# Weight tiles at eight different byte offsets in a residual block on one core

## The chip, the cores and the metric

The kernel runs on one core of one Trainium2 chip. The metric is the device time of one execution in microseconds; lower is better. TensorE (PE) multiplies, VectorE (DVE) and ScalarE (ACT) do elementwise work, GpSimd (POOL) a little of it, and SyncE (SP) issues most DMAs. PEld is TensorE's loading of the operand that stays in the array while the other streams past.

## The reference

One residual block over 256 tokens of width 1024, all in float32:

```python
h = rmsnorm(x, ffn1_pre_g)
x = x + 0.5 * rmsnorm(swiglu(h, ffn1_w_in, ffn1_w_down), ffn1_post_g)
h = rmsnorm(x, mix_pre_g)
q_a, f_a, i_a, g_a, q_b, k_b, v_b, f_b, gates = split(h @ w_in)
y_a = (rmsnorm(hgrn2_chunkwise(q_a, f_a, i_a, lb), hg_norm_g) * silu(g_a)) @ w_branch_a
y_b = fox_attention(q_b, k_b, v_b, f_b + fox_f_bias) @ w_branch_b
y = sigmoid(gate_0) * y_a + sigmoid(gate_1) * y_b
x = x + rmsnorm(y @ w_out, mix_post_g)
x = x + rmsnorm(mem_cross_attention(rmsnorm(x, mem_pre_g), rmsnorm(mem, mem_kv_g)), mem_post_g)
h = rmsnorm(x, ffn2_pre_g)
x = x + 0.5 * rmsnorm(swiglu(h, ffn2_w_in, ffn2_w_down), ffn2_post_g)
```

The two feed-forward parts have an inner width of 2816. `hgrn2_chunkwise` is a gated linear recurrence with 8 heads, `fox_attention` a causal attention with a forgetting bias and 8 heads, and the memory read has 4 heads over 256 memory rows.

## The kernel before

All weights lie in DRAM as 261 units of 128 rows by 1024 float32 words (512 KB each). `unit` (L112) brings one in: a DMA from SP's queue into a buffer `raw` (4 of these), a ScalarE copy (L121) that rounds it to the format float32r as `hi`, and a VectorE subtraction (L122) that puts the rest, raw - hi, into `lo`. There are 8 buffers each for `hi` and `lo`. These two tiles are the "two parts" of a unit. Units are numbered in the order of the table `_ORDER` (L49); most of them are asked for in fours (`chunk`, L126). The numbers run from 0 (first feed-forward block) to 260.

Activations are split in the same way and held transposed by the class `Pair` (L138): tiles `hT` and `lT` of 128 partitions with four blocks of 256 tokens. A product of activations and weights is then three matmuls per block, hi by hi, hi by lo and lo by hi, added up in PSUM. Two forms carry nearly all of them:

- weights streamed, activations loaded (`proj_tok`, L156, `act_first`, `down`, `rows_proj`): 512 columns of `hi` or `lo` stream past a loaded 128 by 128 block of `hT`, `lT` or `act`. In the rows of the profile the streamed operand stands first behind the arrow: `mm<-hi,hT ... 128x512`.
- activations streamed, weights loaded (`proj_col`, L165): 256 columns of `hT` or `lT` stream past a loaded 128 by 128 block of `hi` or `lo`: `mm<-hT,hi ... 128x256`.

Every such matmul is issued by the helper `MM` (L78 and L79), so its line is L79 whichever part of the block it belongs to. The stages run one after the other in the reference's order; small pieces of work (transposes, products of the recurrence, norms) are put at given places among the matmuls by `after` (L82), which counts issued matmuls. The gated recurrence (class `Rec`, `products` and `grow`) multiplies unrounded float32 tiles `k` and `q` in 32 by 32 pieces at the levels m = 0, 1, 2, 4, 8, 16, 32, 64 and 128; for m below 32 it takes the columns whose position has a given bit set (`odd`), so at m = 1 every second word, at m = 16 a plain run of 16 words.

The first input is X1 (L397): the tokens of x, transposed by the host and multiplied by the gain of the first norm (`gain_split`, L241), from tiles `xT` whose blocks are 257 words long because a gain stands behind each. X1 is the loaded operand in the first feed-forward block.

Data tiles of the pool `data` (tag `m4`: hT, lT, act, k, q, f and others) share 21 buffers of equal size, and a buffer has the size of the largest tile of its tag: 4096 bytes a partition. Buffers of `hi` and `lo` have 4096 bytes too. As laid out, the first `hi` buffer begins at byte 47136 of each partition, the first `lo` buffer at 79904, the first `m4` buffer at 112672, and all of these are 2080 modulo 4096.

Of the kernel before, what the change touches and what calls it, by code (L numbers as in the profile page):

```python
# [10 lines left out]
F32R = mybir.dt.float32r  # L11
# [5 lines left out]
P = 128  # L17
D = 1024
T = 256
# [24 lines left out]
WARM = 7  # L44

X_AT = 6


_ORDER = [  # L49
# [15 lines left out]
def block_kernel(ctx: ExitStack, tc: tile.TileContext, wts, x_in, xT_in, mem_in, memT_in, cols, rows, fbias, masks, out):  # L65
# [4 lines left out]
    wp = ctx.enter_context(tc.tile_pool(name="weights", bufs=4))  # L70
# [18 lines left out]
    def nm(s):  # L89
        count[0] += 1  # L90
        return f"{s}_{count[0]}"

    def m4(shape, dt=F32, n="m"):
        return mp.tile(shape, dt, tag="m4", name=nm(n))
# [17 lines left out]
    def unit(name, i, parts=1):  # L112
        u = _AT[name] + i
        if u not in cache:
            raw = wp.tile([P, D], F32, tag="raw", name=nm("raw"), bufs=4)
            hi = wp.tile([P, D], F32R, tag="hi", name=nm("hi"), bufs=8)
            lo = wp.tile([P, D], F32R, tag="lo", name=nm("lo"), bufs=8)
            for a in range(0, D, D // parts):
                cut = slice(a, a + D // parts)
                loads.append(nc.sync.dma_start(raw[:, cut], wts[u][:, cut]).ins)  # L120
                S.copy(hi[:, cut], raw[:, cut])  # L121
                V.tensor_tensor(out=lo[:, cut], in0=raw[:, cut], in1=hi[:, cut].bitcast(F32), op=ALU.subtract)  # L122
            cache[u] = (hi, lo)
        return cache[u]

    def chunk(name, c):  # L126
        return [unit(name, 4 * c + i) for i in range(4)]
# [10 lines left out]
    class Pair:  # L138


        def __init__(self, n=2):
            self.h, self.l = [], []
            for _ in range(n):
                self.more()

        def more(self):
            self.h.append(m4([P, 4, T], F32R, "hT"))
            self.l.append(m4([P, 4, T], F32R, "lT"))

        def hi(self, kb, a=0, b=T):  # L150
            return self.h[kb // 4][:, kb % 4, a:b]
# [89 lines left out]
    def gain_split(X, kb, src, g, a=0, b=T, first=False):  # L241
        gs = cols_s[:, g + kb : g + kb + 1] if isinstance(g, int) else g
        if first:
            V.tensor_scalar(out=X.hi(kb, a, b), in0=src, scalar1=gs, scalar2=None, op0=ALU.mult)
        else:
            S.activation(X.hi(kb, a, b), src, AF.Copy, scale=gs)  # L246
        V.scalar_tensor_tensor(out=X.lo(kb, a, b), in0=src, scalar=gs, in1=X.hi(kb, a, b).bitcast(F32), op0=ALU.mult, op1=ALU.subtract)  # L247
# [39 lines left out]
    def ffn(w_in, w_dn, X, r2, n_tok, i_row, first_half, second_half=None):  # L287
# [44 lines left out]
        def down(c, h):  # L332
            act = acts[c]
            hs = slice(h * P, (h + 1) * P)
            for j in range(2):
                wh, wl = unit(w_dn, 2 * c + j)
                ah, al = act[:, 0, j, hs], act[:, 1, j, hs]
                for n in range(2):
                    ns = slice(n * 512, (n + 1) * 512)
                    for i, (a, w) in enumerate(((ah, wh), (ah, wl), (al, wh))):  # L340
                        MM(accs[h][n], a, w[:, ns], start=(c == 0 and j == 0 and i == 0), stop=(c == NFF - 1 and j == 1 and i == 2))
# [51 lines left out]

    X1 = Pair()
    xT = [m4([P, 2, T + 1], n="xT") for _ in range(KB // 2)]  # L397
    for kb in range(2):
        S.dma_start(xT[0][:, kb], xT_in[:, kb])
# [7 lines left out]
    for j in range(4):  # L407
        unit("f1_in", j, 2 if j == 0 else 1)
        for i in range(2):
            gain_split(X1, 2 * j + i, xT[j][:, i, :T], xT[j][:, i, T:], first=2 * j + i == 0)  # L410

    def norm_1():
        with tc.issue_after(loads[X_AT]):
            for h in range(2):
                nc.sync.dma_start(xs[:, h], x_in[:, h])
        with tc.issue_after(loads[-1]):
            nc.sync.dma_start(cols_s, cols)
            nc.sync.dma_start(fb_s, fbias)
            nc.sync.dma_start(masks_s, masks)
        return [rstd_x(x_halves(h)) for h in range(2)]  # L420
# [4 lines left out]
    def half(X, r, h, g, m):  # L425

        with after(m):
            to_T(X, x_blocks(h), h, g)
        r[h] = rstd_x(x_halves(h))

    ffn("f1_in", "f1_dn", X1, norm_1, 0, 0, lambda m: half(X2, r2, 0, G_MIX, m + L_F1))

# [51 lines left out]
    for c in range(2):  # L484
        u = chunk("f_a", c)
# [12 lines left out]
    for c in range(2):  # L498
        u = chunk("q_a", c)
# [109 lines left out]
    for c in range(2):  # L609
        u = chunk("g_a", c)  # L610
# [9 lines left out]
    for c in range(2):  # L620
        for name, lst, sc in (("k_b", kb_, 1.0), ("q_b", qb_, 1.0 / math.sqrt(128.0))):
            u = chunk(name, c)
# [114 lines left out]
    for c in range(2):  # L737
        u = chunk("v_b", c)
# [87 lines left out]
    for c in range(2):  # L826
        u = chunk("mk", c)
# [9 lines left out]
    for c in range(2):  # L837
        u = chunk("mq", c)
# [165 lines left out]
```

## Time and profile before

| | |
|---|---|
| median of 2 executions | 812.25 us (812.25 to 812.26) |
| profiled execution | 812.33 us |
| its span, first to last instruction | 810.5 us |
| granted TensorE clock, mean | 0.997 |
| PE busy | 795.7 us (98%), 5408 matmuls |
| PEld busy | 698.1 us (86%) |
| DVE busy | 523.6 us (65%) |
| ACT busy | 415.0 us (51%) |
| weight DMAs | 260 of 512 KB, 4.5 us each from issue to landing |
| first unit | two halves |

How to read it: matmuls are pipelined, so the duration in a row holds the latency of the array, and the rows of two neighbours overlap. What a matmul costs a stream of its kind is the distance from its start to the next one's start. A float32 product that isn't of the rounded format stands in the trace as two records. A group's row gives line, engine, operation, output and inputs, shape, count, then busy time and mean ns of one, then idle time of the engine just before and what ended it.

### The profile page before, as it was taken

Reading aid. Unit: us, or ns where it says so; the run is one execution under the profiler, and the core shown is the slowest. Engines: PE = TensorE matmul, PEld = TensorE weight load, DVE = VectorE, ACT = ScalarE, POOL = GpSimd, SP = SyncE. Lnnn points to the kernel's source line nnn. Section 1 sums busy time; section 2 is a strip of 40 time slices with the busy share of each in tenths; the row PEclk is TensorE's granted clock in tenths of the full one; section 3 lists DMA queues with packets and bytes.
Section 4 is the critical chain, followed back from the end, with each engine's and each line's share of the span. In section 5 each row is a group of like instructions: output and inputs, shape, how many; then the busy total and the mean of one; then the engine's idle time right before and its main releaser. Section 6 shows DMA issues by size and latency. Waiting matters only on the chain.

```text
span 810.5 us, 13507 instructions
## 1 busy us (share of the span) xinstructions
PE 795.7 (98%) x5408; PEld 698.1 (86%) x5408; DVE 523.6 (65%) x837; ACT 415.0 (51%) x635; POOL 8.8 (1%) x20
## 2 busy tenths in 40 slices
PE   8999999999999999999999999999999999999996
PEld 6888888888899889998999998999987788888884
DVE  6864545539767896678585566975748755544544
ACT  6754445436754425348675335744647654534531
POOL 0000000000000100100000000000000000000000
PEclk9999999999999999999999999999999999999998
DMA  8866654645555464643467457455426656654521
GB/s 314 294 220 216 211 187 157 198 165 191 169 187 193 137 206 141 205 140 128 133 232 233 155 162 233 156 180 203 143 79 202 208 175 202 213 201 170 182 79 52
DMA packets 41294, 146.91 MB, mean 181 GB/s; under 512 B 4744, under 2 KB 5136, under 8 KB 41232
## 3 DMA queue, kind: packets, MB, share of 16 engines
q1 hardware_dynamic: 40048, 143.42, 52.7%
q0 software_dynamic: 464, 1.58, 0.7%
q10 hardware_dynamic: 720, 1.05, 0.4%
q8 instruction: 42, 0.69, 0.3%
q14 instruction: 20, 0.16, 0.1%
HBM read 144.98 MB, written 1.06 MB: 180 GB/s over the span
## 4 chain that ended last, share of the span: by engine, by line
PE 89%; DVE 4%; DMA 2%; issue 2%; ACT 1%; SPq 0%; DVEq 0%; ACTq 0%
PE mm L79 63%; PE acc L79 23%; DMA raw<-in_wts_dram 2%; DVE lo L122 2%; PE tr L302 1%; PE tr L79 1%; ACT junk L218 1%; DVE xs L282 1%; PE tr L255 1%; DVE t L207 1%; DVE y L209 0%; ACT hi L121 0%; DVE post L278 0%; PE tr L711 0%; PE tr L881 0%
## 5 line engine op out<-in xcount | busy, mean ns | idle before, releaser
L122 DVE TENSOR_TENSOR lo<-raw,hi 128x1024 fp32r<-128x1024 f32 (+1 forms) x262 | 317.2, 1221 | 95.0 <-ACT hi L121 86.0
L121 ACT CAST hi<-raw 128x1024 fp32r<-128x1024 f32 (+1 forms) x262 | 269.0, 1047 | 115.2 <-PE mm L79 77.7
L79 PE MATMUL mm<-hT,lo 128*128 128x256 f32 x648 | 183.8, 284 | 0.8 <-issue 0.8
L79 PE MATMUL mm<-hT,hi 128*128 128x256 f32 x648 | 183.7, 284 | 0.0
L79 PE MATMUL mm<-lT,hi 128*128 128x256 f32 x648 | 183.7, 283 | 0.0
L79 PE MATMUL mm<-lo,hT 128*128 128x512 f32 x448 | 175.9, 393 | 0.0
L79 PE MATMUL mm<-hi,hT 128*128 128x512 f32 x448 | 175.6, 392 | 0.0
L79 PE MATMUL mm<-hi,lT 128*128 128x512 f32 x448 | 175.0, 391 | 0.4 <-DVE lT L247 0.4
L79 PEld LDWEIGHTS mm<-hT,lo 128*128 128x128 f32 x648 | 124.3, 192 | 1.1 <-issue 1.0
L79 PEld LDWEIGHTS mm<-lT,hi 128*128 128x128 f32 x648 | 124.3, 192 | 0.1
L79 PEld LDWEIGHTS mm<-hT,hi 128*128 128x128 f32 x648 | 124.3, 192 | 0.1
L79 PE MATMUL acc<-hi,act 128*128 128x512 f32 x352 | 111.6, 390 | 0.0
L79 PEld LDWEIGHTS mm<-hi,lT 128*128 128x128 f32 x448 | 84.2, 188 | 18.4 <-DVE lT L247 1.1
L79 PEld LDWEIGHTS mm<-hi,hT 128*128 128x128 f32 x448 | 84.1, 188 | 17.9 <-ACT hT L246 0.5
L79 PEld LDWEIGHTS mm<-lo,hT 128*128 128x128 f32 x448 | 84.2, 188 | 16.7
L79 PEld LDWEIGHTS acc<-hi,act 128*128 128x128 f32 x352 | 66.2, 188 | 13.4
L79 PE MATMUL acc<-lo,act 128*128 128x512 f32 x176 | 70.1, 398 | 0.0
L307 ACT ACTIVATE sg<-mm,rstd 128x256 f32<-128x256 f32 x40 | 19.0, 475 | 76.1 <-PE mm L79 76.1
L309 DVE SCALAR_TENSOR_TENSOR at<-mm,rstd,sg 128x256 f32<-128x256 f32 x40 | 19.2, 480 | 58.5 <-ACT sg L307 58.5
L79 PEld LDWEIGHTS acc<-lo,act 128*128 128x128 f32 x176 | 33.1, 188 | 6.3
L79 PE MATMUL acc<-hi,hT 128*128 128x512 f32 x96 | 35.3, 395 | 2.0 <-ACT hi L121 1.4
L79 PE MATMUL acc<-hi,lT 128*128 128x512 f32 x96 | 35.2, 393 | 0.5 <-DVE lT L247 0.5
(175 smaller groups left out, 630.1 us busy)
## 6 DMA issues: line engine op xcount, KB each, us to landing
raw<-in_wts_dram SPq DMA_DIRECT2D x260, 512.0 KB, 4.5
grow<-in_rows_dram SPq DMA_DIRECT2D x4, 512.0 KB, 5.8
xs<-in_x_dram SPq DMA_DIRECT2D x2, 512.0 KB, 5.6
cbm<-cd POOLq DMA_DIRECT2D x2, 512.0 KB, 6.8
memT<-in_memT_dram SPq DMA_DIRECT2D x2, 512.0 KB, 6.6
ms<-in_mem_dram SPq DMA_DIRECT2D x2, 512.0 KB, 6.6
out_dram<-xs SPq DMA_DIRECT2D x4, 256.0 KB, 2.0
xT<-in_xT_dram ACTq DMA_DIRECT2D x3, 257.0 KB, 6.7
```

Source lines behind the costliest of these rows:

```text
L79: log.append(PE.matmul(*args, **kw).ins)
L121: S.copy(hi[:, cut], raw[:, cut])
L122: V.tensor_tensor(out=lo[:, cut], in0=raw[:, cut], in1=hi[:, cut].bitcast(F32), op=ALU.subtract)
L207: V.scalar_tensor_tensor(out=t, in0=v, scalar=y, in1=y, op0=ALU.mult, op1=ALU.mult)
L218: S.activation(junk[:, : src.shape[-1]], src, AF.Square, accum_out=dst)
L255: PE.transpose(ps[:, j * P : (j + 1) * P], src(kb), ident)
L282: V.scalar_tensor_tensor(out=xh, in0=t, scalar=r, in1=xh, op0=ALU.mult, op1=ALU.add)
L302: PE.transpose(trv[:, j, h * P : (h + 1) * P], ats[c, h][:, j * P : (j + 1) * P], ident)
L307: S.activation(sg, ps[:, :FC], AF.Silu, scale=r2[h])
L309: V.scalar_tensor_tensor(out=a, in0=ps[:, FC:], scalar=r2[h], in1=sg, op0=ALU.mult, op1=ALU.mult)
```

## The change

Each unit gets an offset from a table by its number modulo 8: 0, 1, 2, 4, 8, 16, 24 or 32 words, that is 0, 4, 8, 16, 32, 64, 96 or 128 bytes. The buffers of `hi` and `lo` become 32 words longer (4224 bytes), and both parts of the unit are views of 1024 words that begin at the offset. `raw` is as before. X1 alone gets blocks of 260 words in place of 256, of which 256 are used, so its blocks stand 1040 bytes apart. As its tiles are now the largest of tag `m4`, all 21 buffers of that tag become 4160 bytes long. The instructions on every engine, their order and what each waits for stay as they were; only addresses differ.

```diff
+W_OFF = (0, 1, 2, 4, 8, 16, 24, 32)
...
             raw = wp.tile([P, D], F32, tag="raw", name=nm("raw"), bufs=4)
-            hi = wp.tile([P, D], F32R, tag="hi", name=nm("hi"), bufs=8)
-            lo = wp.tile([P, D], F32R, tag="lo", name=nm("lo"), bufs=8)
+            off = W_OFF[u % 8]
+            hi = wp.tile([P, D + 32], F32R, tag="hi", name=nm("hi"), bufs=8)[:, off : off + D]
+            lo = wp.tile([P, D + 32], F32R, tag="lo", name=nm("lo"), bufs=8)[:, off : off + D]
...
-        def __init__(self, n=2):
-            self.h, self.l = [], []
+        def __init__(self, n=2, pad=0):
+            self.h, self.l, self.pad = [], [], pad
...
-            self.h.append(m4([P, 4, T], F32R, "hT"))
-            self.l.append(m4([P, 4, T], F32R, "lT"))
+            self.h.append(m4([P, 4, T + self.pad], F32R, "hT"))
+            self.l.append(m4([P, 4, T + self.pad], F32R, "lT"))
...
-    X1 = Pair()
+    X1 = Pair(pad=4)
```

## The prediction

> **What bounds the kernel now.** I read the engine totals first, then the chain that ended last, then the groups of matmuls by form, and last the chain in order of time, for the distance from one matmul to the next. First the engine totals and the chain by engine and line, from the page:
>
> ```profile
> span 810.5 us, 13507 instructions
> PE 795.7 (98%) x5408; PEld 698.1 (86%) x5408; DVE 523.6 (65%) x837; ACT 415.0 (51%) x635; POOL 8.8 (1%) x20
> PE 89%; DVE 4%; DMA 2%; issue 2%; ACT 1%; SPq 0%; DVEq 0%; ACTq 0%
> ```
>
> TensorE is on the path for 89% of the span. The change leaves every instruction, its order and its waits as they are, so the whole question is whether an instruction takes another time when an operand begins at another address. The groups by form give the counts (last columns: busy us, mean ns of one):
>
> ```profile
> L79 PE MATMUL mm<-hT,lo 128*128 128x256 f32 x648 | 183.8, 284 | 0.8 <-issue 0.8
> L79 PE MATMUL mm<-hT,hi 128*128 128x256 f32 x648 | 183.7, 284 | 0.0
> L79 PE MATMUL mm<-lT,hi 128*128 128x256 f32 x648 | 183.7, 283 | 0.0
> L79 PE MATMUL mm<-lo,hT 128*128 128x512 f32 x448 | 175.9, 393 | 0.0
> L79 PE MATMUL mm<-hi,hT 128*128 128x512 f32 x448 | 175.6, 392 | 0.0
> L79 PE MATMUL mm<-hi,lT 128*128 128x512 f32 x448 | 175.0, 391 | 0.4 <-DVE lT L247 0.4
> L79 PE MATMUL acc<-hi,act 128*128 128x512 f32 x352 | 111.6, 390 | 0.0
> L79 PE MATMUL acc<-lo,act 128*128 128x512 f32 x176 | 70.1, 398 | 0.0
> L79 PE MATMUL acc<-hi,hT 128*128 128x512 f32 x96 | 35.3, 395 | 2.0 <-ACT hi L121 1.4 <-ACT hT L246 0.4
> L79 PE MATMUL acc<-hi,lT 128*128 128x512 f32 x96 | 35.2, 393 | 0.5 <-DVE lT L247 0.5
> L79 PE MATMUL acc<-lo,hT 128*128 128x512 f32 x96 | 34.9, 391 | 0.0
> ```
>
> Weights (hi, lo) stream past loaded activations in 3x448 + 352 + 176 + 3x96 = 2160 matmuls of 512 columns; weights are the loaded operand in 3x648 = 1944 matmuls of 256. The means hold the pipeline's latency; the path pays the distance from start to start. Two pieces of the chain in order of time (start us, length us, what) hold one kind each: 48 matmuls of 512 columns in the first feed-forward block, 84 of 256 in the memory keys:
>
> ```profile
> 64.32 10.89 PE mm L79 x48
> 409.98 10.08 PE mm L79 x84
> ```
>
> So 10.89/48 = 226.9 ns per matmul of 512 and 10.08/84 = 120.0 ns per matmul of 256. The difference, 106.9 ns for 256 columns, is 0.418 ns a column; what is left is a fixed 226.9 - 512x0.418 = 13.1 ns per matmul in both. 2160x0.2269 + 1944x0.1200 = 723 us is 89% of the span, the chain's own figure for PE. An effect of addresses would have to sit in the 0.418 ns a column or in the 13.1 ns.
>
> **The change part by part.** The profiled execution took 812.33 us, 1.8 us of it outside its span of 810.5 us; the median is 812.25 us, so the sum may be made against either.
>
> (1) The streamed weights. Before, each buffer is 4096 bytes a partition, so all hi, lo and activation blocks begin at the same place modulo 512 bytes (32 bytes past a multiple of 64, as the pools lie). After, a unit begins 0, 4, 8, 16, 32, 64, 96 or 128 bytes into a buffer of 4224, an eighth of the units each: about 2160/8 = 270 matmuls of 512 per offset. No matmul of the rounded kind (hi, lo, hT, lT) is now streamed from an odd place, so I bound its price by neighbours. The nearest rows are the 32x32 products of the gated recurrence. At the level m=1 the streamed columns are every second word beginning one word in (4 bytes off); at m=16 they are a plain run beginning 64 bytes in. The two bursts of 128 records, in the timeline:
>
> ```profile
> 276.17 1.29 PE L79 MATMUL acc<-q,k 128*32 128x16 f32 x128
> 300.32 1.32 PE L79 MATMUL acc<-q,k 128*32 128x16 f32 x128
> ```
>
> 1.29 against 1.32 us: beginning at an odd word costs at most nothing measurable. That is unrounded data at 16 columns, a weak witness for a stream of 512, so the price keeps two ends. Upwards, the largest difference between two like forms in the groups above is 8 ns (acc<-lo,act 398, acc<-hi,act 390). If each matmul that meets the two odd offsets (4 and 8 bytes) paid it, a quarter of 2160 streamed and of 1944 loaded, (540 + 486) x 8 ns = 8.2 us: 820.5 us. Downwards, if that common start is itself bad and the fixed 13.1 ns came from it, the two offsets that mend it (32 and 96 bytes) would save 540 x 13.1 ns = 7.1 us: 805.2 us. I take 0, the value of the nearest row.
>
> (2) The loaded weights, and the loaded first input. Loading 32 and 128 columns takes:
>
> ```profile
> L79 PEld LDWEIGHTS acc<-q,k 128*32 128x32 f32 x832 | 8.5, 110 | 2.4 <-issue 1.8 <-PE mm L79 0.4
> L79 PEld LDWEIGHTS mm<-hT,hi 128*128 128x128 f32 x648 | 124.3, 192 | 0.1
> ```
>
> (192 - 110)/96 = 0.85 ns a column, 109 ns for 128 columns. Beside a matmul of 512 (226.9 ns) that has room to double; beside one of 256 (120.0 ns) only 11 ns are free. That is the cover of this part: it hides a few ns, not a slow load. The blocks of the first input (loaded in the first feed-forward block, next to streams of 512) now stand 1040 bytes apart instead of 1024, always on multiples of 16 bytes, and because that pool gives each buffer the size of its largest tile, all its 21 buffers move to a distance of 4160 bytes. I take 0 for both; the 8.2 us above hold the upper end of the weights.
>
> (3) The two instructions that write each unit, and the scale and subtraction that write the first input:
>
> ```profile
> L122 DVE TENSOR_TENSOR lo<-raw,hi 128x1024 fp32r<-128x1024 f32 x260 | 315.9, 1226 | 95.0 <-ACT hi L121 86.0
> L121 ACT CAST hi<-raw 128x1024 fp32r<-128x1024 f32 x260 | 267.8, 1050 | 114.6 <-PE mm L79 77.7 <-DMA raw<-in_wts_dram 20.2 <-PE acc L79 12.4
> L574 DVE TENSOR_TENSOR q<-q,f 128x512 f32<-128x512 f32 x2 | 1.4, 688 | 0.7 <-PE acc L79 0.7
> L798 DVE TENSOR_TENSOR zg<-zg,zg 128x512 f32<-128x512 f32 x4 | 2.8, 688 | 0.1
> ```
>
> L574 with f writes every second word from an odd word on, L798 a plain run: 688 ns both, so I take 0 for VectorE. For reads there are the blocks of xT, every second one of which begins 1028 bytes after the first, against those of memT, which all begin evenly (min/median/max):
>
> ```profile
> L247 DVE SCALAR_TENSOR_TENSOR lT<-xT,hT x8: 475/478/486, 5.7 to 15.4; 128x256 fp32r<-128x256 f32 x8
> L246 ACT ACTIVATE hT<-xT x7: 494/502/505, 6.7 to 13.9; 128x256 fp32r<-128x256 f32 x7
> L246 ACT ACTIVATE hT<-memT,cols_s x8: 494/495/508, 405.5 to 408.4; 128x256 fp32r<-128x256 f32 x8
> L247 DVE SCALAR_TENSOR_TENSOR lT<-memT,cols_s,hT x8: 475/476/477, 406.7 to 409.4; 128x256 fp32r<-128x256 f32 x8
> ```
>
> No difference beyond 7 ns. A ScalarE write at an odd word has no row. If it doubled CAST for a quarter of the units, 65 x 1.05 = 68 us of ScalarE work would be added, and most of it is covered: eight buffers run ahead, as the waits show (us in total, times, longest):
>
> ```profile
> ACT hi L121 <- PE mm L79: 77.7, 79, 7.6
> PE acc L79 <- ACT hi L121: 1.4, 1, 1.4
> ```
>
> ScalarE waits for TensorE to free a buffer far longer than the reverse. Without that cover, at the head, units 1 and 2 would each come 1.05 us later: 2.1 us, 814.4 us. I take 0. The DMAs (raw has no offset), PSUM, the queues of SP and POOL and every wait stay where they are.
>
> Sum: 812.3 + 0 + 0 + 0 = **812.3 us**.
>
> **The rivals.**
>
> *A stream that begins at an odd word goes at half pace* (slower; decided by whether words are taken in pairs). Offset 4 bytes alone would split each pair. Price: 270 matmuls x 512 columns x 0.418 ns = 57.8 us, all on the path: 870.1 us. If loads halved as well, 243 x 0.109 = 26 us more. For it: the trace has no rounded stream at an odd start. Against it: the m=1 burst above, and that it needs a pace that breaks over the whole stream, not at its start.
>
> *One more group of words per stream* (slower, inside 2%). If words are taken in groups of four, offsets 4 and 8 bytes straddle one group more: 540 streams x 4 x 0.418 ns = 0.9 us, and, where no room is left beside 256 columns, 486 loads x 4 x 0.85 ns = 1.7 us: 814.9 us. For it: these are the only two offsets that are no multiple of 16 bytes. Against it: a hidden prefetch would swallow 1.7 ns, and no row shows such a step. [...]
>
> *The fixed 13.1 ns is a collision* (faster). If the stream and the load that runs beside it meet because both begin at the same phase, giving them different phases removes it for up to seven units in eight: (2160 + 1944) x 7/8 x 13.1 ns = 47 us, 765.3 us. For it: the same 13.1 ns in both sizes, as one load runs beside each. Against it: a place where the load comes late. Timeline, both queues of TensorE:
>
> ```profile
> 160.44 0.39 PE L79 MATMUL mm<-hi,lT 128*128 128x512 f32 x1
> 160.44 0.19 PEld L79 LDWEIGHTS mm<-hi,hT 128*128 128x128 f32 x1
> 160.67 0.39 PE L79 MATMUL mm<-hi,hT 128*128 128x512 f32 x1
> 160.88 0.20 PEld L302 LDWEIGHTS tr<-ident,at 128*128 128x128 f32 x2 [0.25 <-DVE at L309]
> 160.89 0.43 PE L302 MATMUL tr<-ident,at 128*128 128x128 f32 x2
> ```
>
> The matmul at 160.67 has no load beside it until 160.88, and its successor still starts 0.22 us later, as that of the matmul at 160.44 does (0.23), which had one. So the 13.1 ns does not come from the load. [...]
>
> **How the numbers follow.** No effect of addresses at all: 0.65, 812.3 us. One more group: 0.13, 814.9 us. The late head, 814.4 us: 0.03. The mended start, 805.2 us: 0.04. These four lie within 2% (796.0 to 828.5 us), which is about what a measurement of this kernel can tell from no change: 0.85. Half pace: 0.11, 870 us and more: slower. Collision removed: 0.04, 765 us: faster. The range is that of the four cases within 2% with the bounds of part 1, 805 to 821 us; they hold 0.85, so no more than 2 in 10 is left out without the two far cases.
>
> **What would show it.** Right: in the profile after, pieces of 48 matmuls of 512 still take 10.89 us and of 84 of 256 still 10.08 us, whatever the unit; the groups of L79, L121 and L122 (L81, L124 and L125 in the changed file) keep their means within a few ns. Half pace would show as one unit in eight with some 440 ns from start to start; one more group as 1 to 4 ns on two units in eight; a collision removed as 214 and 107 ns from start to start on most units. The prediction is wrong if any group of matmuls shifts by more than 8 ns a piece, or if TensorE begins to wait for hi or lo, which it now does for 1.4 us.

## The result and the profile after

The changed kernel takes 819.18 us (818.79 to 819.57) against 812.25 us: a ratio of 1.009 with a 95% interval of 1.007 to 1.011. That lies inside the predicted range of 805 to 821 us, but 6.9 us above the predicted 812.3, and the difference is no noise: the likeliest case of the prediction, no effect of addresses at all, did not happen.

Engine totals and the chain by engine, from the page of the changed kernel:

```profile
span 817.0 us, 13507 instructions
PE 805.0 (99%) x5408; PEld 698.5 (85%) x5408; DVE 523.9 (64%) x837; ACT 415.4 (51%) x635; POOL 9.1 (1%) x20
PE 94%; DVE 2%; DMA 1%; issue 1%; ACT 1%; ACTq 0%; DVEq 0%
```

VectorE and ScalarE are busy as long as before (523.6 and 415.0 us). TensorE's share of the chain rose from 89% to 94%; that would be some 45 us, far more than the time grew, because the chain is laid through other engines less often (VectorE 2% of it against 4%, DMA 1% against 2%), so the price has to be read from the matmuls. The groups by form (busy us, mean ns of one) say which matmuls grew:

```profile
L81 PE MATMUL mm<-hT,lo 128*128 128x256 f32 x648 | 182.8, 282 | 0.5 <-issue 0.5
L81 PE MATMUL mm<-lo,hT 128*128 128x512 f32 x448 | 178.1, 398 | 0.0
L81 PE MATMUL acc<-hi,act 128*128 128x512 f32 x352 | 113.5, 396 | 0.0
```

These of 512 columns grew by 5 to 6 ns (393 to 398, 390 to 396), those of 256 shrank by 2 (284 to 282). The chain in order of time gives the path's own price, the distance from start to start:

```profile
65.19 11.19 PE mm L81 x48
405.56 81.94 PE mm L81 x692
```

The first is the piece that took 10.89 us before. The second took, before:

```profile
402.18 83.03 PE mm L79 x692
```

11.19/48 = 233.1 ns where it was 226.9, and 81.94/692 = 118.4 ns where it was 120.0. Over the whole trace, the distances that follow a rounded matmul of 512 columns sum to 512.3 us (501.9 before), those that follow one of 256 to 244.4 us (247.7), all the rest of the span to 60.3 us (60.9): +10.4 - 3.3 - 0.6 = +6.5 us, the growth of the span. So the whole time sits in the matmuls themselves. Setting each matmul of the trace against the unit that it streams, waits left out, units 4 bytes in take 236.6 ns, units 8 bytes in 233.3, and all others 231.8 to 232.5, the units at offset 0 among them. The offsets are therefore not the whole story: a unit that still begins at the start of its buffer is also slower.

### The profile page after: what moved, and what is told of

Read it like the earlier page. It is cut to its first block, busy times and chain, and to the rows that moved or that the text cites. A ratio compares the mean times of both kernels' runs of the same rounds, so it can differ in the third digit from the quotient of the medians.

```text
span 817.0 us, 13507 instructions
## 1 busy us (share of the span) xinstructions
PE 805.0 (99%) x5408; PEld 698.5 (85%) x5408; DVE 523.9 (64%) x837; ACT 415.4 (51%) x635; POOL 9.1 (1%) x20
## 4 chain that ended last, share of the span: by engine, by line
PE 94%; DVE 2%; DMA 1%; issue 1%; ACT 1%; ACTq 0%; DVEq 0%
PE mm L81 64%; PE acc L81 26%; DMA raw<-in_wts_dram 1%; PE tr L305 1%; PE tr L81 1%; PE tr L258 1%; DVE lo L125 1%; DVE xs L285 0%; PE tr L714 0%; ACT hi L124 0%; DVE t L210 0%; ACT junk L221 0%; PE tr L884 0%; DVE y L212 0%; DVE post L281 0%
## 5 line engine op out<-in xcount | busy, mean ns | idle before, releaser
L81 PE MATMUL mm<-lo,hT 128*128 128x512 f32 x448 | 178.1, 398 | 0.0
L81 PE MATMUL mm<-hi,hT 128*128 128x512 f32 x448 | 177.8, 397 | 0.0
L81 PE MATMUL mm<-hi,lT 128*128 128x512 f32 x448 | 177.3, 396 | 0.0
L81 PEld LDWEIGHTS mm<-hT,lo 128*128 128x128 f32 x648 | 122.1, 188 | 0.8 <-issue 0.7
L81 PEld LDWEIGHTS mm<-hT,hi 128*128 128x128 f32 x648 | 122.3, 189 | 0.1
L81 PEld LDWEIGHTS mm<-lT,hi 128*128 128x128 f32 x648 | 122.2, 189 | 0.2
L81 PE MATMUL acc<-hi,act 128*128 128x512 f32 x352 | 113.5, 396 | 0.0
```

Source lines behind the costliest of these rows:

```text
L81: log.append(PE.matmul(*args, **kw).ins)
```

## The experiments

Theories. W: the weights' addresses cost the time. A: the data buffers, which now stand 4160 bytes apart, cost it. Both were rivals at first; later S (a matmul is short while phases do not change from one to the next) stood against D (the difference between the streamed and the loaded operand's address sets each matmul's time). "Phase" is the address modulo 256 or 512 bytes. Behind each measured time stands the ratio to the kernel before, with its interval. The two pieces shown each time are those above: 48 matmuls of 512 columns in the first feed-forward block (at 65 or at 83 us; all such pieces of one kernel lie within 0.15 us), 692 of 256 in the gates and the two branch products. (The prediction's 84 matmuls of 256 at 410 us lie in the gates too, not in the memory keys; the 120.0 ns stay right.)

### Half of the change at a time

The weights' part alone (`X1 = Pair()` in the changed kernel):

```diff
-    X1 = Pair(pad=4)
+    X1 = Pair()
```

> The weights' offsets and longer buffers alone; the first input keeps blocks of 1024 bytes, so the 21 data buffers are 4096 bytes apart again. Theory W (the weights' addresses cost the 7 us): 818 to 820 us, matmuls of 512 columns at about 232 ns. Theory A (the data buffers' new distance of 4160 bytes costs it): 812 to 814 us, 227 ns apart from the units at 4 bytes (some 5 ns more).

Measured: 818.63 us, 1.0076 (1.0061 to 1.0091).

```profile
65.36 11.18 PE mm L81 x48
405.72 81.74 PE mm L81 x692
```

The first input's part alone:

```diff
-            off = W_OFF[u % 8]
-            hi = wp.tile([P, D + 32], F32R, tag="hi", name=nm("hi"), bufs=8)[:, off : off + D]
+            off = 0
+            hi = wp.tile([P, D], F32R, tag="hi", name=nm("hi"), bufs=8)[:, off : off + D]
...
```

> The padded first input alone; every weight unit begins at its buffer's start, buffers 4096 bytes. Theory A (the data buffers' new distance of 4160 bytes): 817 to 819 us, 232 ns per matmul of 512 columns and 118 per one of 256. Theory W (the weights' addresses): 812 to 813 us, 227 and 120 ns.

Measured: 817.78 us, 1.0062 (1.0045 to 1.0079).

```profile
82.22 11.09 PE mm L81 x48
404.84 82.34 PE mm L81 x692
```

Each theory gave the right time for its own half, and both fall as the sole cause: either half alone costs 5 to 6 us, both together 6.9 and not 11. Whatever was good before is lost by the first of the two.

### Buffers further apart without offsets, and all units at an odd word

In the changed kernel, the offsets and the longer input blocks are taken out, and the longer weight buffers stay:

```diff
-            off = W_OFF[u % 8]
+            off = 0
...
-    X1 = Pair(pad=4)
+    X1 = Pair()
```

> Weight buffers of 4224 bytes with all units at offset 0, data buffers 4096 bytes apart as before: the distances between weight buffers change, the offsets do not. If the distance of the buffers is what costs: 817 to 819 us, 232 ns per matmul of 512 columns. If only the offsets inside the buffers cost: 812 to 813 us, 227 ns.

Measured: 817.44 us, 1.0059 (1.0044 to 1.0074). The distance between buffers is enough. With `off = 1` in place of 0:

> Every unit 4 bytes into a buffer of 4224 bytes, the first input not padded. If an odd start costs its own 4 to 5 ns per streamed matmul of 512 (237 against 232 ns in the changed kernel): 2160 x 5 ns = 10 us over the kernel with long buffers at offset 0. If the units at 4 bytes were slow only by their place in the mix: the same time as that kernel.

Measured: 826.50 us, 1.0169 (1.0153 to 1.0184), 9.1 us over the one at offset 0. The piece of 48, first with offset 0, then with 4 bytes:

```profile
64.86 11.09 PE mm L81 x48
```

```profile
83.99 11.33 PE mm L81 x48
```

231.0 against 236.0 ns (the six such pieces of the first block take 11.06 to 11.09 us and 11.30 to 11.38 us): beginning at an odd word cost some 5 ns a matmul more here.

### One common difference

The kernel before, with unused bytes between weights and data buffers:

```diff
+            if not cache:
+                V.memset(wp.tile([P, 16], F32, tag="shim", name="shim", bufs=1), 0.0)
             cache[u] = (hi, lo)
```

> The kernel before with 64 unused bytes between the weight buffers and the data buffers (one small VectorE memset is added): all weights keep one phase and all data buffers keep one phase, 64 bytes apart. Theory S (a matmul is short while the phases do not change from one matmul to the next): 812 to 813 us, 227 and 120 ns from start to start. Theory D (the difference between the streamed and the loaded phase sets each matmul's time): 815 to 821 us, one steady value of 230 to 235 ns for 512 columns, without spread.

Measured: 818.42 us, 1.0069 (1.0054 to 1.0084).

```profile
82.92 11.20 PE mm L79 x48
405.70 81.50 PE mm L79 x692
```

With 128 bytes (`[P, 32]`):

> As the last, with 128 bytes in place of 64. Theory S: 812 to 813 us, 227 and 120 ns. Theory D: a steady value near that of units 128 bytes off in the kernel with long buffers, 232 ns for 512 columns, 818 us or more.

Measured: 820.21 us, 1.0090 (1.0075 to 1.0105).

```profile
82.53 11.20 PE mm L79 x48
406.03 83.04 PE mm L79 x692
```

S falls. All weights keep one phase here and all data buffers another, nothing changes from one matmul to the next, and still the pieces of 48 `mm` take 11.20 us (233.3 ns; one of 11.15 with 128 bytes). D holds. One part of its expectation missed: the distances are not without spread, they alternate between some 231 and 236 ns with 64 bytes and between 229 and 238 with 128.

The kernel with long buffers at offset 0, whose weight buffers stand 128 bytes out of step, shows both levels side by side. In its piece of 48 at 81.95 us, ten matmuls in a row take 229 and 237 or 238 ns in turn, as with 128 unused bytes; then come three of 231 to 232 ns, then nine of 226 to 227, as in the kernel before. If the two levels are the differences of 128 and of 0, the difference sets the distance of single matmuls too, and the three between them, some 5 ns above the lower level, are what a change of phase cost: that much of S may be left. Which unit lies at which phase is inferred here from the distances; the trace shows no addresses.

### How many address bits count, and again the odd word

The kernel before with buffers of `[P, D + 64]`, 4352 bytes:

> The kernel before with weight buffers 4352 bytes apart, all units at offset 0: phases are equal modulo 256 bytes, but not modulo 512. If only the address modulo 256 or less counts: 812 to 813 us and 227 ns. If more address bits count: 814 to 818 us with matmuls of 512 columns spread from 226 to 236 ns, as with buffers 4224 apart.

Measured: 812.69 us, 0.9994 (0.9982 to 1.0006).

```profile
64.31 10.89 PE mm L79 x48
402.64 83.03 PE mm L79 x692
```

The buffers are 256 bytes out of step modulo 512, and all is as before: of the addresses tried, only the part modulo 256 counts (a difference of 128 bytes does count: 233.3 ns for 512 columns in the run above). The same with each unit 4 bytes in (`[:, 1 : 1 + D]`):

> As the last, each unit 4 bytes into its buffer. If an odd start has a price of its own, on top of the phases: 4 to 6 ns for each of 2160 matmuls, 9 to 13 us over the kernel with buffers 4352 apart. If what cost in the kernel with all units at 4 bytes was the mixture of phases: no more than 2 us over it.

Measured: 828.66 us, 1.0193 (1.0177 to 1.0208), 16.0 us over the last, more than the 9 to 13 expected, since equal phases were lost as well (4.8 of the 10.4 ns a matmul, by the run after this one).

```profile
66.69 11.39 PE mm L79 x48
411.89 81.89 PE mm L79 x692
```

The same with each unit 16 bytes in separates the two:

> Buffers 4352 bytes apart, every unit 16 bytes in: a difference of 16 bytes modulo 256 for every pair. If a difference of 16 bytes counts like one of 64: 230 to 234 ns for 512 columns, 816 to 820 us. If only differences of 32 or 64 bytes count: 812 to 813 us. If the price of 4 bytes came from unequal phase alone, this would cost as much as the odd start, 828 us.

Measured: 816.86 us, 1.0053 (1.0037 to 1.0068).

```profile
65.01 11.12 PE mm L79 x48
404.88 83.04 PE mm L79 x692
```

The first case came true: a difference of 16 bytes costs 231.7 - 226.9 = 4.8 ns per matmul of 512, much like one of 64, and one of 4 bytes 237.3 - 226.9 = 10.4 ns. No run moves both operands by 4 bytes, so it stays open whether the additional 5.6 ns go with the difference or with the odd start itself.

### The difference, or the place?

The kernel before with the same 64 unused bytes ahead of all weight buffers, so that raw, weights and data buffers all move together:

```diff
+            if not cache:
+                V.memset(wp.tile([P, 16], F32, tag="shim", name="shim", bufs=1), 0.0)
             raw = wp.tile([P, D], F32, tag="raw", name=nm("raw"), bufs=4)
```

> The kernel before with 64 unused bytes ahead of all weight buffers, so that raw, weights and data buffers all move by 64 bytes and the differences stay. If the difference of the two operands is what counts: 812 to 813 us, 227 and 120 ns. If the absolute place modulo 256 counts: about 818 us, as when the data buffers alone moved by 64.

Measured: 812.32 us, 0.9996 (0.9987 to 1.0005).

```profile
64.20 10.88 PE mm L79 x48
402.39 83.03 PE mm L79 x692
```

Moving everything by 64 bytes costs nothing, moving one side by 64 costs 5.4 us (818.42 against 812.99 us in its set of runs). For a move of 64 bytes, it is the difference.

### A version that uses it

A difference of 64 bytes shortens the matmuls of 256 columns (117.8 against 120.0 ns). So only the units that are loaded beside streams of 256 get an offset, in buffers of 4352 bytes (the streams of 512 keep equal phase modulo 256):

```diff
+BY_COLS = ("f_b", "f_a", "q_a", "k_b", "q_b", "gates", "br_a", "br_b", "mk", "mq")
...
+            o = 48 if name in BY_COLS else 0
...
-            hi = wp.tile([P, D], F32R, tag="hi", name=nm("hi"), bufs=8)
-            lo = wp.tile([P, D], F32R, tag="lo", name=nm("lo"), bufs=8)
+            hi = wp.tile([P, D + 64], F32R, tag="hi", name=nm("hi"), bufs=8)[:, o : o + D]
+            lo = wp.tile([P, D + 64], F32R, tag="lo", name=nm("lo"), bufs=8)[:, o : o + D]
```

> Weight buffers 4352 bytes apart; the units whose weights are the loaded operand (1944 matmuls of 256 columns) begin 192 bytes in, all others at 0, so that the streamed operand of those matmuls lies 64 bytes past the loaded one modulo 256, as in the kernel with 64 unused bytes. Theory D: 118 ns for these, 227 ns kept for those of 512 columns: 1944 x 2.1 ns = 4 us saved, 808 to 809.5 us. Theory S' (any two phases in use disturb the matmuls of 512 columns too): 813 us or more.

Measured: 808.40 us, 0.9950 (0.9938 to 0.9963), as D had it. The matmuls of 256 take the 117.8 ns that they took when the data buffers were moved instead, and S' falls, since those of 512 keep 10.89 us.

```profile
64.29 10.89 PE mm L81 x48
401.28 81.51 PE mm L81 x692
```

With `o = 16`, 64 bytes:

> As the first of this set with 64 bytes in place of 192: the streamed operand of the matmuls of 256 columns lies 192 bytes past the loaded one modulo 256. If any unequal phase shortens them: 118 ns, 808 to 809.5 us. If the direction counts: 119.5 to 121 ns, 812 to 815 us.

Measured: **801.72 us, 0.9872 (0.9856 to 0.9887)**, faster than either expectation.

```profile
64.26 10.89 PE mm L81 x48
397.25 78.44 PE mm L81 x692
```

78.44/692 = 113.4 ns, 6.6 ns less than before, with the streams of 512 untouched. The direction does count (113.4 ns at 192 bytes, 117.8 at 64), but neither case had the right sign for it. 1944 x 6.6 = 12.8 us would be the gain if all stages had it; the trace's distances after matmuls of 256 fall by 10.3 us and the span by 10.3 us (810.5 to 800.2). This version beats both kernels.

Start to start, in ns, by the address of the streamed operand less that of the loaded one, modulo 256 (from the pieces above):

| difference, bytes | 512 columns | 256 columns |
|---|---|---|
| 0 | 226.9 | 120.0 |
| 4 | 237.3 | |
| 16 | 231.7 | |
| 64 | | 117.8 |
| 128 | 233.3 | 120.0 |
| 192 | 233.3 | 113.4 |
| 240 | | 120.0 |
| 252 | | 118.3 |

## Why the prediction was right or wrong, step by step

*The frame held, the range by luck.* Instructions, order and waits did not move, TensorE's matmuls set the time (94% of the chain), and an effect of addresses had to sit in their spacing. The time lies inside the range, but not by the path that the prediction gave. Its upper end, 820.5 us, stands for 8 ns on a quarter of the matmuls, those that meet the two odd offsets, and the 8 ns were the difference of two like forms in a kernel where all pairs have equal phase: no measure of addresses. In fact the streams of 512 grew by some 5 to 6 ns at the other offsets and by 10 at 4 bytes (+10.4 us, 0.5 of it in the first 40 matmuls), and those of 256, for which no case but the far collision had a gain, shrank (-3.3 us). That the sum of the two fell inside the range is luck.

*Its own signs spoke against it.* Pieces of 48 were to stay at 10.89 us; they take 11.12 to 11.25. A shift of any group by more than 8 ns was to show it wrong; three groups shift so:

```profile
L81 PE MATMUL acc<-hi,hT 128*128 128x512 f32 x96 | 36.7, 410 | 1.0 <-ACT hi L124 0.9
L81 PE MATMUL acc<-hi,lT 128*128 128x512 f32 x96 | 36.3, 406 | 0.0
L81 PE MATMUL acc<-lo,hT 128*128 128x512 f32 x96 | 35.8, 401 | 0.0
```

They had 395, 393 and 391 ns. Much of this is the head: in this execution the first matmuls stand some 427 ns apart until 9.8 us. That costs nothing by itself, as the 41st matmul with weights starts at 16.83 us against 16.88 before. The wait for hi, the other sign, did not grow (0.9 us against 1.4).

*Part 1 failed: "I take 0, the value of the nearest row."* The burst of 16-column products at m = 1 did not stand for a rounded stream of 512: its 128 records are unrounded and pass in 1.29 us, 10 ns each. More important, the part asked only where the streamed operand begins. What counts is where it begins relative to the loaded one (818.42 us with one side moved by 64 bytes, 812.32 with both), and in the kernel before that difference is 0 modulo 256 for every rounded matmul, so no row of one could show it. The term taken as 0 measured +10.4 us for the streams of 512 and -3.3 us for those of 256, over the whole change.

*Part 2 failed in the same way.* It took 0 for the data buffers' new distance of 4160 bytes. The run with the first input's part alone gives 5.0 us for it (817.78 against 812.75 us in the same set of runs), although no weight moved. Its remark that loads have room only beside streams of 512 played no part: the groups of loads of 128 columns of hi, lo, hT, lT and act take 188 to 192 ns in the kernel before and 188 to 194 in the changed one.

*Part 3 was right.* Subtractions and casts at odd words cost nothing. VectorE and ScalarE rows of the kernel with every unit 4 bytes in, where the kernel before had 1226 and 1050 ns:

```profile
L122 DVE TENSOR_TENSOR lo<-raw,hi 128x1024 fp32r<-128x1024 f32 x260 | 316.4, 1228 | 100.7 <-ACT hi L121 100.3
L121 ACT CAST hi<-raw 128x1024 fp32r<-128x1024 f32 x260 | 267.6, 1050 | 118.2 <-PE mm L79 78.9 <-DMA raw<-in_wts_dram 20.6 <-PE acc L79 15.8
```

*The rivals.* Half pace did not happen: an odd word costs 10.4 ns of 226.9, not 214. One more group of words was too small: 4 bytes cost 5.6 ns more than 16 bytes, where the prediction's group of four words would take 1.7 ns (four columns of 0.418 ns, its estimate), and a multiple of 16 bytes is not free: at a difference of 16 bytes the streams of 512 take 231.7 ns against 226.9. The hidden prefetch held against it is a supposition that no run shows. The collision that the new phases were to remove had its sign right for 256 columns (120.0 to 113.4 ns at best) and wrong for 512, where equal phase (226.9 ns) is the best of those tried.

*The late load.* The argument that the fixed 13.1 ns does not come from a load running beside the stream was sound (0.22 us with none beside it, 0.23 with one), and one place suggests the same for the new part. In the kernel with long buffers at offset 0, a load that comes late (timeline, both queues):

```profile
639.61 0.40 PE L81 MATMUL mm<-hi,lT 128*128 128x512 f32 x1
639.83 0.20 PEld L305 LDWEIGHTS tr<-ident,at 128*128 128x128 f32 x2 [0.25 <-DVE at L312]
639.85 0.42 PE L305 MATMUL tr<-ident,at 128*128 128x128 f32 x2
```

Nothing loads beside the matmul at 639.61, and its successor still starts 0.24 us later, as against 0.22 in the kernel before. But the conclusion that phases could then not matter went too far: the runs above show that they do. By what mechanism stays open. The trace does not show reads inside an instruction, and differences other than those of the table were not tried on their own.

## What to carry to other kernels

Where TensorE bounds the time, the distance from one matmul's start to the next is worth reading to the nanosecond: 5 ns on 2160 matmuls were 10 us here. A layout in which all rows share one alignment shows nothing of what another alignment costs, and zero is then no safe reading: bound it by a real experiment or keep both signs. Moving one operand of each kind by 64 bytes, or making a tile that shares its pool 64 bytes longer, is a cheap trial in either direction.

## What the runs showed of the hardware

In these runs the spacing of rounded float32 matmuls with a loaded block of 128 by 128 followed the difference of the two operands' addresses modulo 256 bytes: 226.9 to 237.3 ns for 512 columns, 113.4 to 120.0 ns for 256. A further 256 bytes between buffers changed nothing (812.69 against 812.99 us), nor did moving both operands together by 64 bytes (812.32 against 812.75 us). Equal phase is the best case found for 512 columns (226.9 ns); for 256, where 64, 192 and 252 bytes shorten it (117.8, 113.4 and 118.3 ns), nothing longer than its 120.0 ns was found in the gates and branch products. Where all pairs have one difference of 64 or 128 bytes, the distances alternate between two values (231 and 236, 229 and 238 ns), and the pieces of 48 `mm` repeat to within 0.05 us (11.15 to 11.20). ScalarE and VectorE at work made no difference to them: in the changed kernel the mean for 512 columns was 232.8 ns with both idle and 232.7 ns with a cast and a subtraction running throughout.
